# Stores of activations on SP, ten slots, shared wide buffers and early buffers beside the output projection

## The chip, the cores and the metric

The kernel runs on one core of a Trainium2 chip. The metric is device time in microseconds (us) of one execution, lower is better. The core has a matrix engine (TensorE, "PE" in the profile, with its weight loads as "PEld"), three engines for elementwise work (VectorE "DVE", ScalarE "ACT", GpSimd "POOL") and one that only issues transfers (SyncE "SP"). Every engine runs its own instructions strictly in order and waits on semaphores for the others. POOL, too, issues transfers, among them those that add to what lies at the destination ("accumulate").

## The reference

One decoder block on x of 512 tokens by 2048 channels, all in fp32. The part that matters here is the second half: the output projection of the mixers, and the gated MLP with its causal convolution of width 3.

```python
mix = concatenate([y_rwkv, y_pool]) @ w_out          # 2048 x 2048
x = x + gt1 * mix
h = rmsnorm(x, norm2_g) * (1 + sc2) + sh2

u = h @ w_up                                          # 2048 x 11264
y = conv_b + sum(conv_w[j] * shift(u, 2 - j) for j in range(3))
val, gate = split(y, 2)
x = x + gt2 * ((silu(gate) * val) @ w_down)           # 5632 x 2048
return rmsnorm(x, norm_f_g)
```

Ahead of it stand adaLN from c, the input projection, an RWKV-7 scan and a causal pooling mixer. None of that is touched.

## The kernel before

Channels lie on the 128 partitions and the 512 tokens in the free dimension; H0 and H1 are the two halves of 256 tokens. Each fp32 product is made of three matmuls (`mm3`, L118 to L122): operands are split into a rounded high part and the rest, and high×high (L120), high×low (L121) and low×high (L122) are summed in PSUM. So each weight tile needs a cast on ScalarE and a subtraction on VectorE before PE may use it: L113 and L115 for the earlier projections, L844 (`uhi`) and L846 (`ulo`) in `wsplit` for the up- and down-projection.

The stages, in the profile's time: the mixers up to some 785 us; the output projection (L769 to L818) up to some 985; the up-projection with convolution up to 2090; the down-projection to the end. The code is written as one stream, and a scheduler lays it out on the engines: it decides, per engine, in which order instructions stand, from which data and buffers they need. A pool's tag names a buffer; a new tile with a tag waits until the last user of the old one is done.

**Output projection.** `out_half(hf, f)` makes 128 output channels for one token half: four chunks of weights, each split by L113 and L115, then the residual and a store of x2 by POOL (L767). Loads of the mixers' outputs (`mxl`, L673) and their casts (`ah`, L141) feed it.

**Up-projection.** 88 blocks of 128 columns, in NF = 44 pairs j (a value block and its gate block). A pair's weights are two rows of 1 MB of `wup` (`row`, L855 to L860), row 0 = (w11, w12) and row 1 = (r1 base, w22), in four buffers x2_0 to x2_3 taken in turn, two per pair. So row 1 of one pair goes where row 1 of the pair two earlier lay, and may be loaded when its last reader, the subtraction of w22, is done. Each pair takes seven products in a scheme in the manner of Strassen, of 24 matmuls each: w11·Y11, w12·Y21, r1·T1, r2·T2, r4·Y22, r3·T3 and w22·T4. The activations T1 to T4, Y11, Y21, Y22 are sums and differences of h's quarters, split once (`combos`, L881 to L904). The weights' sums are made on the fly: r1 is row 1's right half plus an accumulate transfer by POOL (L967); r2 = r1 + w11 (VectorE, L991); r4 = r2 + w12 (L998); r3 is loaded by SP (L969) and accumulated by POOL (L970). w22·T4 of a pair is done in the next pair's iteration (`last_product`), since its row comes last; behind it `finish_pair` (L933 to L944) convolves u1 and u2 (L927 to L929), applies silu on ScalarE (L940), multiplies (L941), and POOL stores the result to `ad` in DRAM (L943). Partial sums leave PSUM by copies on ScalarE (L980, L989, L996; `cap`) and adds on VectorE (L985, L1000, L1009). These use `Slot`, a list of free buffers of 128×512 taken in the order in which they came free.

For the first NB = 10 pairs the first two products need only the first token half, so `first_two` (L866 to L877) makes them ahead, keeps them in DRAM (`early`), and the pair's iteration reads them back (L975) and takes five products instead of seven.

**Down-projection.** Two halves of 22 blocks; `act_pair` (L1027 to L1038) loads pairs of blocks of `ad`, casts (L1034) and subtracts (L1035) them into buffers freed by the up-projection (`ATAGS`); `down` loads weight rows (L1051) and splits them with `wsplit`.

Of the kernel before, what the change touches and what calls it, by code (L numbers as in the profile page):

```python
# [9 lines left out]
F32 = mybir.dt.float32  # L10
F32R = mybir.dt.float32r
# [5 lines left out]
P = 128  # L17
T = 512
D = 2048
KT = D // P  # L20
# [2 lines left out]
NC = 4  # L23
WC = 512
NWF = 8
NSLOT = 6
NB = 10
NJ = NF // 2
Q = float(np.exp(-0.5))
# [26 lines left out]
def block_kernel(ctx, tc, a, out, stop=None, dbg=None):  # L56
    nc = tc.nc
    V, S, G, PE = nc.vector, nc.scalar, nc.gpsimd, nc.tensor
# [65 lines left out]
    def project(ps, src, acts, start=True, stop=True, engs=(V,)):  # L124

        n = len(acts)
        for k0 in range(0, n, WC // P):
            wh, wl = split_weights(src[:, k0 * P : k0 * P + WC], engs[k0 // 4 % len(engs)])
            for kk in range(WC // P):
                k = k0 + kk  # L130
                sl = slice(kk * P, (kk + 1) * P)
                last = mm3(ps, wh[:, sl], wl[:, sl], *acts[k], start=start and k == 0, stop=stop and k == n - 1)
        return last
# [43 lines left out]
    if True:  # L177
# [28 lines left out]
        for k in range(KT):  # L206
            for part in (1, 0):
                j = part * 16 + k
# [9 lines left out]
            hi, lo = slots(k)  # L218
# [450 lines left out]
    M = []  # L669
# [35 lines left out]
    def half(acts, hf):  # L705
        sl = slice(hf * HT, (hf + 1) * HT)
        return [(h[:, sl], l[:, sl]) for h, l in acts]

    def wide(name):

        return rb.tile([P, 4, HT], F32, tag="wide", name=name, bufs=3)
# [57 lines left out]
    for f in range(8):  # L769
        out_done(f, pss[f], 0, T)  # L770

    def out_half(hf, f):
        ps = bank()[:, 0:HT]
        project(ps, a["wout"][f, :, :], half(M, hf))
        out_done(f, ps, hf * HT, (hf + 1) * HT)


# [7 lines left out]
    def split4(pool, tag, src):  # L785

        t = pool.tile([P, 2, 4, HT], F32R, tag=tag, name=tag)
        S.copy(t[:, 0, :, :], src)
        V.tensor_tensor(t[:, 1, :, :], src, t[:, 0, :, :].bitcast(F32), op=ALU.subtract)
        return t  # L790
# [13 lines left out]
    for f in range(8, KT):  # L804
        if f == 9:
            dg = norm_rows(acc[:, H0])
        if f == 10:
            rstd = norm_bcast(dg)
        if f >= 10:
            next(steps, None)  # L810
            if f % 2:
                next(steps, None)
        out_half(1, f)
    hctx.close()
    if stop == "B":
        return
# [11 lines left out]
    class Slot:  # L828
# [9 lines left out]
        def done(self):  # L838
            free.append(self.home)

    def wsplit(src):
        n = src.shape[-1]
        hi = ub.tile([P, 2 * QW], F32R, tag="whi", name="uhi", bufs=3)
        S.copy(hi[:, 0:n], src)  # L844
        lo = ub.tile([P, 2 * QW], F32R, tag="wlo", name="ulo", bufs=3)
        V.tensor_tensor(lo[:, 0:n], src, hi[:, 0:n].bitcast(F32), op=ALU.subtract)  # L846
        return hi, lo

# [8 lines left out]
    def row(n, pool, tag):  # L857
        t = pool.tile([P, 4 * QW], F32, tag=tag, name="wrow")
        nc.sync.dma_start(t, a["wup"][n, :, :])
        return t  # L860
# [4 lines left out]

    def first_two(n):  # L866

        w = row(2 * n, ub, f"t4{n % 2}")
        s_ = Slot("u1")
        ps = bank()[:, 0:HT]  # L870
        product(ps, w[:, W1], Y11)
        S.copy(s_[:, H1], ps)
        ps = bank()[:, 0:HT]
        product(ps, w[:, W2], Y21)
        V.tensor_add(s_[:, H0], s_[:, H1], ps)
        G.dma_start(early[n], s_.t)
        s_.done()  # L877
# [3 lines left out]
    def combos():  # L881
        for g in range(2):
            normed(g, H1, rstd)
            yield
            t = wide("t1")
            V.tensor_sub(t, x2q[g][:, :, H0], x2q[g][:, :, H1])
            T1[g] = split4(ub, f"t1{g}", t)
            yield
        for g in range(2):
            normed(g + 2, H1, rstd)  # L890
            yield
            t3 = wide("t3")
            V.tensor_sub(t3, x2q[g + 2][:, :, H1], x2q[g][:, :, H1])
            t2 = wide("t2")
            V.scalar_tensor_tensor(t2, t3, -1.0, x2q[g][:, :, H0], op0=ALU.mult, op1=ALU.subtract)
            yield
            T2[g] = split4(ub, f"t2{g}", t2)
            T3[g] = split4(ub, f"t3{g}", t3)
            yield
            Y22[g] = split4(ub, f"y22{g}", x2q[g + 2][:, :, H1])  # L900
            V.scalar_tensor_tensor(t2, t2, -1.0, x2q[g + 2][:, :, H0], op0=ALU.mult, op1=ALU.subtract)
            t4.append(t2)
            yield
# [12 lines left out]
    for _ in steps:  # L916
        pass
    for g in range(2):
        T4[g] = split4(ub, f"t4{g}", t4[g])
    free.append((rb, "acc"))  # L920

    ncw = rb.tile([P, 3, NF], F32, tag="ncw", name="ncw")
# [10 lines left out]
    def finish_pair(j, u1, u2):  # L933
        yv, yg = Slot("yv"), Slot("yg")
        conv(u1.t, yv.t, col("cw", j), col("cw", 88 + j), col("cw", 176 + j), col("cb", j))
        u1.done()

        conv(u2.t, yg.t, ncw[:, 0, j : j + 1], ncw[:, 1, j : j + 1], ncw[:, 2, j : j + 1], col("cb", 44 + j))
        u2.done()
        S.activation(yg.t, yg.t, AF.Silu)  # L940
        V.tensor_mul(yv.t, yv.t, yg.t)  # L941
        yg.done()
        G.dma_start(ad[j], yv.t)  # L943
        yv.done()  # L944

    pend = None
# [13 lines left out]
    for j in range(NF):  # L960
        w = []
        for i in range(2):
            w.append(row(2 * j + i, rb, f"x2_{(0, 2, 1, 3)[rows % 4]}"))
            rows += 1

        w11, w12, r1, w22 = w[0][:, W1], w[0][:, W2], w[1][:, W1], w[1][:, W2]
        G.dma_start(r1, a["wup"][2 * j + 1, :, W2], accum_op=ALU.add)  # L967
        r3 = ub.tile([P, 2 * QW], F32, tag="wr", name="r3", bufs=2)
        nc.sync.dma_start(r3, a["wup"][2 * j, :, W1])  # L969
        G.dma_start(r3, a["wup"][2 * j + 1, :, W1], accum_op=ALU.add)  # L970
        pa = bank()[:, 0:HT]
        cap = Slot("cap")
        if j < NB:
            u1 = Slot("u1")
            G.dma_start(u1.t, early[j])  # L975
            if pend:
                last_product(pend)
        else:
            product(pa, w11, Y11)
            S.copy(cap[:, H0], pa)  # L980
            last_product(pend)
            u1 = Slot("u1")
            pb = bank()[:, 0:HT]
            product(pb, w12, Y21)
            V.tensor_add(u1[:, H0], cap[:, H0], pb)  # L985
        u2 = Slot("u2")
        pc = bank()[:, 0:HT]
        product(pc, r1, T1)
        S.copy(cap[:, H1], pc)  # L989
        r2 = wide("r2").rearrange("p a b -> p (a b)")  # L990
        V.tensor_add(r2, r1, w11)  # L991
        product(pa, r2, T2, start=j < NB)
        if j < NB:
            V.tensor_add(cap[:, H0], u1[:, H1], pa)
        else:
            S.copy(cap[:, H0], pa)  # L996
        r4 = wide("r4").rearrange("p a b -> p (a b)")
        V.tensor_add(r4, r2, w12)  # L998
        product(pc, r4, Y22, start=False)
        V.tensor_add(u1[:, H1], cap[:, H0], pc)  # L1000
        if j < NB:
            pd = bank()[:, 0:HT]
            product(pd, r3, T3)
            V.tensor_add(u2[:, H1], cap[:, H0], cap[:, H1])
            V.tensor_add(u2[:, H1], u2[:, H1], pd)
            pend = (j, u1, u2, pd, w22, cap)
        else:
            product(pa, r3, T3, start=False)
            V.tensor_add(u2[:, H1], cap[:, H1], pa)  # L1009
            cap.done()  # L1010
            pend = (j, u1, u2, pa, w22, None)
# [10 lines left out]
        V.scalar_tensor_tensor(jk, wa, 1.0, cb, op0=ALU.mult, op1=ALU.mult, accum_out=mod[:, 80 + i : 81 + i])  # L1022

    ATAGS = [(rb, "y0"), (rb, "y1"), (rb, "y2"), (rb, "y3")]
    ATAGS += [(ub, f"{t}{g}") for t in ("t1", "t2", "y22", "t3", "t4") for g in range(2)]

    def act_pair(i):  # L1027

# [12 lines left out]
    def down_row():  # L1041
        nrow[0] += 1
        if nrow[0] % 5 < 2:
            return ub.tile([P, 2 * QW], F32, tag="wr", name="wd", bufs=2)
        return wide("wd").rearrange("p a b -> p (a b)")

    def down(ps, f, h, acts, blocks=(0, 8, 16)):
# [9 lines left out]
    def down_four(h, acts):  # L1057

        pss = [bank() for _ in range(4)]
        for k0 in (0, 8, 16):  # L1060
            for f in range(4):
                down(pss[f], f, h, acts, (k0,))
        return pss

    yd = [tc.dram_tile([P, T], F32, name=f"yd{f}") for f in range(KT)]
    A = []
    for i in range(NJ // 2):
        A += act_pair(i)
    for f in range(KT):
        if f == 0:  # L1070
            pss = down_four(0, A)
        ps = pss[f] if f < 4 else bank()
        if f >= 4:
            down(ps, f, 0, A)
        s_ = Slot("yd")
        S.copy(s_.t, ps)
        G.dma_start(yd[f], s_.t)
        s_.done()
        if f < 8:
            ada_gate2(2 * f)  # L1080
            ada_gate2(2 * f + 1)
# [2 lines left out]
    def gate(f):  # L1084
        return mod[:, 80 + f : 81 + f]

    A = []
    for i in range(NJ // 2, NJ):
        A += act_pair(i)
    x2q = [quad(i, "x2") for i in range(4)]  # L1090

    def load_x2(f):
# [140 lines left out]
```

## Time and profile before

| | us |
|---|---|
| median of the 3 runs shown (2594.88 to 2607.85) | 2604.18 |
| the profiled execution, its own time | 2610.18 |
| its span in the trace | 2608.1 |
| DVE waits for accumulated rows at L991 (42 times) | 195.9 |
| PE waits for the copy at L989 (33 times) | 95.3 |

In the profile, a row of an engine's timeline gives the start, the duration, the engine, the line, the operation, out<-in with the shape, and in brackets how long the engine idled before it and what released it. A row of the table of waits gives the waiting instruction, what ended its waits, the total, how many, and the longest.

Names of tiles in the profile lose their numbers, so all of r1's and w22's rows are `wrow`, r2, r3 and r4 are `r`, u1 and u2 are `u`, and a transfer `wrow<-wup` is SP's row load or POOL's accumulate.

### The profile page before, as it was taken

To read this page: it belongs to the slowest core of one execution; us is meant where nothing else is said; L and a number is where in the kernel's file an instruction comes from. 1 tells how busy PE (TensorE), PEld (TensorE's weight loads), DVE (VectorE), ACT (ScalarE), POOL (GpSimd) and SP (SyncE) were. 2 spreads that over 40 slices of the span, in tenths; PEclk is the share of its full clock that TensorE was granted. 3 is DMA by queue.
4 is the path that set the end of the run, shared out by engine and by line. 5 is a ranking of instruction groups with operands and counts; after the bars stand their busy time and mean duration, and the time that the engine had idled before them with its cause. 6 is when DMAs were issued, how large, how long until landed. Compare 5 with 4: busy or idle time off the path is not lost.

```text
span 2608.1 us, 42719 instructions
## 1 busy us (share of the span) xinstructions
PE 2357.0 (90%) x17122; PEld 2042.6 (78%) x17122; DVE 1641.9 (63%) x2648; ACT 1037.5 (40%) x1466; POOL 153.9 (6%) x237
## 2 busy tenths in 40 slices
PE   4789999999999999878889889889898999999997
PEld 3656666666668899777888889889888878877897
DVE  7987777777844567676656656656656674244355
ACT  3243444444333466333344444444444432232242
POOL 0000000000000101111000001001001001010000
PEclk9999999999999999989998999998999999999999
DMA  9965565566636568777555555565565687464365
GB/s 349 340 211 147 149 177 148 164 194 183 180 89 206 177 184 269 202 216 215 150 162 174 143 169 162 153 170 162 153 170 156 192 310 268 135 207 121 104 185 160
DMA packets 210873, 483.05 MB, mean 185 GB/s; under 512 B 73521, under 2 KB 79089, under 8 KB 191217
## 3 DMA queue, kind: packets, MB, share of 16 engines
q1 hardware_dynamic: 187634, 400.62, 48.4%
q0 software_dynamic: 23040, 79.71, 13.0%
q8 instruction: 134, 2.20, 0.3%
q14 instruction: 65, 0.53, 0.1%
HBM read 441.70 MB, written 38.54 MB: 184 GB/s over the span
## 4 chain that ended last, share of the span: by engine, by line
PE 27%; DMA 15%; issue 4%; DVE 4%; ACT 3%; SPq 0%; POOL 0%; ACTq 0%; POOLq 0%; DVEq 0%
DMA wrow<-wup 14%; PE b L120 9%; PE b L121 9%; PE b L122 9%; ACT uhi L844 2%; DVE ulo L846 2%; DVE yg L929 1%; DMA al<-ad 1%; ACT cap L989 0%; DMA yd<-yd 0%; DVE u L985 0%; DVE x L1108 0%; DMA ad<-yv 0%; SPq L1033 0%; DVE yv L941 0%
## 5 line engine op out<-in xcount | busy, mean ns | idle before, releaser
L122 PE MATMUL b<-t,ulo 128*128 128x256 f32 x1408 | 404.6, 288 | 32.1 <-DVE ulo L846 32.1
L120 PE MATMUL b<-t,uhi 128*128 128x256 f32 x1408 | 404.6, 287 | 10.8 <-ACT uhi L844 9.6
L120 PE MATMUL b<-y,uhi 128*128 128x256 f32 x1056 | 323.4, 306 | 97.7 <-ACT cap L989 95.3
L121 PE MATMUL b<-t,uhi 128*128 128x256 f32 x1408 | 403.4, 287 | 0.0
L122 PE MATMUL b<-y,ulo 128*128 128x256 f32 x1056 | 319.0, 303 | 2.2 <-DVE ulo L846 2.2
L121 PE MATMUL b<-y,uhi 128*128 128x256 f32 x1056 | 319.5, 303 | 0.0
L120 PE MATMUL b<-act,uhi 128*128 128x512 f32 (+1 forms) x880 | 307.4, 350 | 9.6 <-ACT act L1034 8.6
L121 PE MATMUL b<-act,uhi 128*128 128x512 f32 (+1 forms) x880 | 307.5, 350 | 0.5 <-DVE act L1035 0.5
L122 PE MATMUL b<-act,ulo 128*128 128x512 f32 (+1 forms) x880 | 307.4, 350 | 0.0
L120 PEld LDWEIGHTS b<-y,uhi 128*128 128x128 f32 x1056 | 222.9, 211 | 104.8 <-ACT cap L989 102.0
L122 PEld LDWEIGHTS b<-t,ulo 128*128 128x128 f32 x1408 | 275.3, 196 | 35.1 <-DVE ulo L846 35.0
L120 PEld LDWEIGHTS b<-t,uhi 128*128 128x128 f32 x1408 | 276.6, 197 | 12.2 <-ACT uhi L844 10.3
L844 ACT CAST uhi<-wrow 128x1024 fp32r<-128x1024 f32 x176 | 183.6, 1049 | 245.6 <-PE b L121 220.2
L121 PEld LDWEIGHTS b<-t,uhi 128*128 128x128 f32 x1408 | 275.5, 196 | 0.0
L846 DVE TENSOR_TENSOR ulo<-wd,uhi 128x1024 fp32r<-128x1024 f32 (+1 forms) x120 | 135.9, 1135 | 210.4 <-ACT uhi L844 201.5
L846 DVE TENSOR_TENSOR ulo<-wrow,uhi 128x1024 fp32r<-128x1024 f32 x176 | 214.8, 1224 | 79.9 <-ACT uhi L844 79.4
L113 ACT CAST whi<-wraw 128x512 fp32r<-128x512 f32 x236 | 145.7, 619 | 291.8 <-PE mm L121 120.4
L844 ACT CAST uhi<-wd 128x1024 fp32r<-128x1024 f32 (+1 forms) x120 | 117.3, 978 | 308.6 <-PE b L121 278.3
L115 DVE TENSOR_TENSOR wlo<-wraw,whi 128x512 fp32r<-128x512 f32 x236 | 161.6, 688 | 118.5 <-ACT whi L113 105.7
L122 PEld LDWEIGHTS b<-y,ulo 128*128 128x128 f32 x1056 | 221.6, 210 | 2.6 <-DVE ulo L846 2.6
L121 PEld LDWEIGHTS b<-y,uhi 128*128 128x128 f32 x1056 | 222.1, 210 | 0.0
L846 DVE TENSOR_TENSOR ulo<-r,uhi 128x1024 fp32r<-128x1024 f32 x132 | 161.2, 1222 | 59.7 <-ACT uhi L844 59.7
(309 smaller groups left out, 4661.3 us busy)
## 6 DMA issues: line engine op xcount, KB each, us to landing
wrow<-wup SPq DMA_DIRECT2D x98, 1024.0 KB, 7.2
wa<-ada SPq DMA_DIRECT2D x48, 1024.0 KB, 7.2
war<-ada SPq DMA_DIRECT2D x192, 256.0 KB, 3.5
wd<-wdn SPq DMA_DIRECT2D x80, 512.0 KB, 4.1
wraw<-win SPq DMA_DIRECT2D x140, 256.0 KB, 4.4
wraw<-wout SPq DMA_DIRECT2D x96, 256.0 KB, 3.4
r<-wup SPq DMA_DIRECT2D x44, 512.0 KB, 3.8
r<-wup POOLq DMA_DIRECT2D x44, 512.0 KB, 9.2
```

Of the source, the lines that this page charges most:

```text
L113: S.copy(hi, raw)
L115: eng.tensor_tensor(lo, raw, hi[:, :].bitcast(F32), op=ALU.subtract)
L120: PE.matmul(ps, wh, xh, start=start, stop=False, skip_group_check=more)
L121: PE.matmul(ps, wh, xl, start=False, stop=False, skip_group_check=more)
L122: return PE.matmul(ps, wl, xh, start=False, stop=stop, skip_group_check=more)
L844: S.copy(hi[:, 0:n], src)
L846: V.tensor_tensor(lo[:, 0:n], src, hi[:, 0:n].bitcast(F32), op=ALU.subtract)
L929: V.scalar_tensor_tensor(y[:, 2:T], u[:, 0 : T - 2], c0, y[:, 2:T], op0=ALU.mult, op1=ALU.add)
```

## The change

Six things are changed. Stores of `ad`, and the read of `early`, are issued by SP in place of POOL. The free list starts with ten slots in place of six (the accumulator's buffer makes eleven). A new pool `ea` is opened before the out-projection's pool closes, and holds two of the three sets of buffers of `wsplit`, and the rows of `first_two`, later T4 and two rows of down weights. r3 is taken from the `wide` buffers that r2 and r4 use, three in all, in place of a pair of its own. `combos` makes its four groups of operands in one loop. In the output projection's last six blocks, the subtraction L115 of every other chunk, twelve in all, stands on GpSimd. In the down-projection, activations are loaded inside `down_four`, eight blocks ahead of their use, and the first four blocks of the second half are loaded during the first.

```diff
-NSLOT = 6
+NSLOT = 10
-    def out_half(hf, f):
+    def out_half(hf, f, engs=(V,)):
-        project(ps, a["wout"][f, :, :], half(M, hf))
+        project(ps, a["wout"][f, :, :], half(M, hf), engs=engs)
-        out_half(1, f)
+        out_half(1, f, (V, G) if f >= 10 else (V,))
+
+    ea = ctx.enter_context(tc.tile_pool(name="ea", bufs=1, reuse_waits="tile"))
     hctx.close()
...
     def wsplit(src):
-        hi = ub.tile([P, 2 * QW], F32R, tag="whi", name="uhi", bufs=3)
+        pool, tag = ((ea, "0"), (ea, "1"), (ub, "2"))[nsplit[0] % 3]
+        nsplit[0] += 1
+        hi = pool.tile([P, 2 * QW], F32R, tag="whi" + tag, name="uhi")
         S.copy(hi[:, 0:n], src)
-        lo = ub.tile([P, 2 * QW], F32R, tag="wlo", name="ulo", bufs=3)
+        lo = pool.tile([P, 2 * QW], F32R, tag="wlo" + tag, name="ulo")
...
-        w = row(2 * n, ub, f"t4{n % 2}")
+        w = row(2 * n, ea, f"t4{n % 2}")
...
             T1[g] = split4(ub, f"t1{g}", t)
             yield
-        for g in range(2):
             normed(g + 2, H1, rstd)
...
-        T4[g] = split4(ub, f"t4{g}", t4[g])
+        T4[g] = split4(ea, f"t4{g}", t4[g])
...
-        G.dma_start(ad[j], yv.t)
+        nc.sync.dma_start(ad[j], yv.t)
...
-        r3 = ub.tile([P, 2 * QW], F32, tag="wr", name="r3", bufs=2)
+        r3 = wide("r3").rearrange("p a b -> p (a b)")
...
-            G.dma_start(u1.t, early[j])
+            nc.sync.dma_start(u1.t, early[j])
...
-    ATAGS += [(ub, f"{t}{g}") for t in ("t1", "t2", "y22", "t3", "t4") for g in range(2)]
+    ATAGS += [(ub, f"{t}{g}") for t in ("t1", "t2", "y22", "t3") for g in range(2)] + [(ea, "t40")]
+    wd2 = ea.tile([P, 2, 2 * QW], F32, tag="t41", name="wd2")
...
-            return ub.tile([P, 2 * QW], F32, tag="wr", name="wd", bufs=2)
+            return wd2[:, nrow[0] % 5, :]
...
         for k0 in (0, 8, 16):
+            while len(acts) < min(k0 + 8, NJ):
+                acts += act_pair((h * NJ + len(acts)) // 2)
             for f in range(4):
                 down(pss[f], f, h, acts, (k0,))
...
-    A = []
-    for i in range(NJ // 2):
-        A += act_pair(i)
+    A, A2 = [], []
...
+        if f == KT - 3:
+            A2 += act_pair(NJ // 2) + act_pair(NJ // 2 + 1)
...
-    A = []
-    for i in range(NJ // 2, NJ):
-        A += act_pair(i)
+    A = A2
```

The new lines shift the numbers by five or six in the up-projection: L846 becomes L852, L928 L933, L941 L946, L985 L990, L991 L996, L998 L1003.

The scheduler places some instructions elsewhere for it. On VectorE, in one iteration of the main up-projection loop, before the change (`yv` and `yg` are the convolved halves of the pair before, the numbers behind names tell tiles apart, r2_16497 belongs to the pair behind, and ulo_16329 is the rest of this pair's r3):

```order
L846 TENSOR_TENSOR ulo_16269<-r2_16265,uhi_16267 128x1024
L928 SCALAR_TENSOR_TENSOR yg_16193<-u2_16002,ncw_10646,yg_16193 128x511
L991 TENSOR_TENSOR r2_16497<-wrow_16358,wrow_16356 128x1024
L929 SCALAR_TENSOR_TENSOR yg_16193<-u2_16002,ncw_10646,yg_16193 128x510
L985 TENSOR_TENSOR u1_16203<-cap_16133,b_16204 128x256
L846 TENSOR_TENSOR ulo_16300<-r4_16296,uhi_16298 128x1024
L941 TENSOR_TENSOR yv_16192<-yv_16192,yg_16193 128x512
L998 TENSOR_TENSOR r4_16528<-r2_16497,wrow_16356 128x1024
L846 TENSOR_TENSOR ulo_16329<-r3_16129,uhi_16327 128x1024
L846 TENSOR_TENSOR ulo_16368<-wrow_16356,uhi_16366 128x1024
```

The same piece of VectorE's order with the change, up to the subtraction of w22 (ulo_16400):

```order
L852 TENSOR_TENSOR ulo_16272<-r2_16268,uhi_16270 128x1024
L933 SCALAR_TENSOR_TENSOR yg_16196<-u2_16005,ncw_10649,yg_16196 128x511
L934 SCALAR_TENSOR_TENSOR yg_16196<-u2_16005,ncw_10649,yg_16196 128x510
L990 TENSOR_TENSOR u1_16206<-cap_16136,b_16207 128x256
L852 TENSOR_TENSOR ulo_16303<-r4_16299,uhi_16301 128x1024
L946 TENSOR_TENSOR yv_16195<-yv_16195,yg_16196 128x512
L996 TENSOR_TENSOR r2_16500<-wrow_16361,wrow_16359 128x1024
L852 TENSOR_TENSOR ulo_16332<-r3_16132,uhi_16330 128x1024
L1003 TENSOR_TENSOR r4_16531<-r2_16500,wrow_16359 128x1024
L852 TENSOR_TENSOR ulo_16371<-wrow_16359,uhi_16369 128x1024
L1005 TENSOR_TENSOR u1_16206<-cap_16136,b_16238 128x256
L852 TENSOR_TENSOR ulo_16400<-wrow_16129,uhi_16398 128x1024
```

r2 of the pair behind, the first reader of the accumulated row, stood third in that piece and now stands seventh: behind both halves of the convolution, u1, the rest of r4 and the product yv. The rest of r3, which came after r4, now stands between r2 and r4.

On SP, with the change, at the loads of the output projection's operands (some 830 us in the profile before):

```order
L673 DMA mxl_8246<-mixd2_102 128x512
L673 DMA mxl_8252<-mixd3_103 128x512
L865 DMA wrow_9930<-wup 128x2048
L673 DMA mxl_8258<-mixd4_104 128x512
L673 DMA mxl_8264<-mixd5_105 128x512
```

The first row of the up-projection's weights (`wrow_9930`) stands between two loads of the mixers' outputs; before the change the loads stood one behind the other, and the row came only after that pool's end. On ScalarE its first cast now stands between those of ah9 and ah10:

```order
L141 CAST ah9_8254<-mxl_8252 128x512
L113 CAST whi_8230<-wraw_8228 128x512
L850 CAST uhi_9934<-wrow_9930 128x1024
L141 CAST ah10_8260<-mxl_8258 128x512
L850 CAST uhi_9964<-wrow_9930 128x1024
```

The casts of the weight row stand ahead of those of ah10 and ah11.

More of the change, by code (lines that the diff above doesn't have):

```diff
@@ L839, in done @@
             free.append(self.home)
+    nsplit = [0]
     def wsplit(src):
         n = src.shape[-1]
-        hi = ub.tile([P, 2 * QW], F32R, tag="whi", name="uhi", bufs=3)
+        pool, tag = ((ea, "0"), (ea, "1"), (ub, "2"))[nsplit[0] % 3]
+        nsplit[0] += 1
+        hi = pool.tile([P, 2 * QW], F32R, tag="whi" + tag, name="uhi")
         S.copy(hi[:, 0:n], src)
-        lo = ub.tile([P, 2 * QW], F32R, tag="wlo", name="ulo", bufs=3)
+        lo = pool.tile([P, 2 * QW], F32R, tag="wlo" + tag, name="ulo")
         V.tensor_tensor(lo[:, 0:n], src, hi[:, 0:n].bitcast(F32), op=ALU.subtract)
```

## The prediction

> **What bounds the kernel now.** I read the page first, then the table of waits, then the stretches, then single iterations.
>
> ```profile
> span 2608.1 us, 42719 instructions
> PE 2357.0 (90%) x17122; PEld 2042.6 (78%) x17122; DVE 1641.9 (63%) x2648; ACT 1037.5 (40%) x1466; POOL 153.9 (6%) x237
> PE 27%; DMA 15%; issue 4%; DVE 4%; ACT 3%; SPq 0%; POOL 0%; ACTq 0%; POOLq 0%; DVEq 0%
> DVE r L991 <- DMA wrow<-wup: 195.9, 42, 7.8
> PE b L120 <- ACT cap L989: 95.3, 33, 5.0
> POOL ad L943 <- DVE yv L941: 416.2, 43, 19.7
> 1269.05:2055.32 786.27, 696.05 (x5377) 689.56 (x5377) 481.05 (x546) 332.48 (x449) 73.04 (x96) 0.93 0.57 161
> ```
>
> PE counts as 90% busy, but a transfer of wup rows is 14 points of the chain, and two waits repeat once per pair: VectorE's add r2 (L991) waits for the accumulated row, and PE's first matmul of the product with r4 waits for the copy L989. The longest wait, POOL's for the store, is no bound: nothing behind it is ready earlier (below). The last row is the main up-projection loop, from the first such PE wait to the last of them: us, busy time of PE, PEld, DVE, ACT, POOL, granted clock, DMA share, GB/s.
>
> ```profile
> 1269.05 0.58 PE L120 MATMUL b<-y,uhi 128*128 128x256 f32 x1 [5.05 <-ACT cap L989]
> 2055.32 0.58 PE L120 MATMUL b<-y,uhi 128*128 128x256 f32 x1 [2.59 <-ACT cap L989]
> 1722.97 0.28 PE L121 MATMUL b<-y,uhi 128*128 128x256 f32 x1
> 1723.09 0.28 PE L122 MATMUL b<-y,ulo 128*128 128x256 f32 x1
> ```
>
> Both ends are the same matmul of pairs 32 iterations apart, so one pair takes 786.27/32 = **24.57 us**. Matmuls start every 0.12 us when nothing stops them; a pair has 7 products of 24, so 168 × 0.12 = **20.16 us** is the least PE can do. The difference, 4.4 us a pair or 141 us in all, is what can be won here. Of it 95.3 us is the wait itself; the rest is the slower clock (0.93 in that row) after each wait.
>
> One iteration, in order of time, shows what closes the circle:
>
> ```profile
> 1694.39 1.23 DVE L846 TENSOR_TENSOR ulo<-wrow,uhi 128x1024 fp32r<-128x1024 f32 x1
> 1695.64 3.32 SPq L859 DMA_DIRECT2D wrow<-wup  x2
> 1701.72 0.85 POOL L967 DMA_DIRECT2D wrow<-wup  x1 [5.42 <-DVE ulo L846]
> 1710.42 1.23 DVE L991 TENSOR_TENSOR r<-wrow 128x1024 f32<-128x1024 f32 x1 [5.45 <-DMA wrow<-wup]
> 1711.57 0.74 DVE L929 SCALAR_TENSOR_TENSOR yg<-u,ncw,yg 128x510 f32<-128x510 f32 x1
> 1712.40 0.63 ACT L940 ACTIVATE yg<-yg 128x512 f32<-128x512 f32 x1 [6.48 <-DVE yg L929]
> 1712.94 1.03 ACT L844 CAST uhi<-r 128x1024 fp32r<-128x1024 f32 x1
> 1713.88 0.36 ACT L989 COPY cap<-b 128x256 f32<-128x256 f32 x1
> 1714.29 0.58 PE L120 MATMUL b<-y,uhi 128*128 128x256 f32 x1 [3.58 <-ACT cap L989]
> 1718.61 1.05 ACT L844 CAST uhi<-wrow 128x1024 fp32r<-128x1024 f32 x1 [3.15 <-PE b L121]
> 1719.69 1.23 DVE L846 TENSOR_TENSOR ulo<-wrow,uhi 128x1024 fp32r<-128x1024 f32 x1 [0.47 <-ACT uhi L844]
> ```
>
> The subtraction for w22 frees a row buffer; SP loads the next odd row into it; POOL accumulates the other row onto its half; r2 may be added: 1710.42 − 1695.62 = 14.8 us. Only then the conv's L929 behind r2 on VectorE, the silu and the cast of r3 behind L929 on ScalarE, the copy L989 behind these, and PE: 3.9 us from r2 to PE. Then 4.3 us of slowed matmuls before a buffer lets the cast of w22 begin, 2.3 us for cast and subtraction, and the ring is closed: 14.8 + 3.9 + 4.3 + 2.3 = 25.3 us (1695.62 to 1720.92). **PE waits for a copy that only stands behind work that waits for a DMA.**
>
> **The change: order of the main loop.** In the changed order r2 stands behind both L929s, the add u1, ulo(r4) and the product yv. So L929, silu, cast and copy no longer wait for the accumulate, and PE's wait at r4 goes. What is late next is the row ring itself, now wholly on VectorE. The rows that price it are the next iteration's r2, VectorE's add u1, and the stretch of the first ten pairs:
>
> ```profile
> 1734.63 1.23 DVE L991 TENSOR_TENSOR r<-wrow 128x1024 f32<-128x1024 f32 x1 [4.41 <-DMA wrow<-wup]
> 1718.80 0.42 DVE L1000 TENSOR_TENSOR u<-cap,b 128x256 f32<-128x256 f32 x1 [1.02 <-PE b L122]
> 1172.00:1251.00 79.00, 65.46 (x496) 63.95 (x497) 51.95 (x68) 29.56 (x36) 11.28 (x16) 0.94 0.72 203
> 1188.65 2.13 SPq L859 DMA_DIRECT2D wrow<-wup  x2
> 1203.36 1.23 DVE L991 TENSOR_TENSOR r<-wrow 128x1024 f32<-128x1024 f32 x1 [4.53 <-DMA wrow<-wup]
> 1208.48 2.13 SPq L859 DMA_DIRECT2D wrow<-wup  x2
> ```
>
> From r2 to the end of ulo(w22) VectorE does r2, ulo(r3), r4, ulo(w11) and ulo(w22), each 1.14 us from start to start (r2 above: 1710.42 to 1711.57), and u1, 0.42 with its overlap taken off 0.35: 6.05 us. The transfer part was 14.8 us above and 13.7 in the next iteration (1720.92 to 1734.63), at 161 GB/s. At a shorter period the same bytes give 161 × 24.57/20.6 = 192 GB/s; the stretch of the first ten pairs has 203 GB/s and took 14.7 us (1188.65 to 1203.36). I take 14.5. Ring: 14.5 + 6.05 = **20.6 us**, just over PE's 20.16. That a ring of this kind sets a pace of its own, that stretch shows: 19.83 us a pair (1188.65 to 1208.48), where five products would let PE do with 120 × 0.12 = 14.4. The gain is 32 × (24.57 − 20.6) = **−127 us**; at PE's own limit −140, and at 22 us (a transfer part of 15.9, over these three) −82.
>
> **Stores of ad on SP.** The 43 waits of 416 us in all leave POOL. They held nothing: at 1701.72 the accumulate starts on its landed row, POOL having idled 5.42 us. On SP the store stands behind the base load of r3 and ahead of the next odd row; it waits for L941, which VectorE now does before r2, while the odd row needs ulo(w22), 6 us after. Nothing; if L941 came late, every us would go into the ring.
>
> **r3 from the wide buffers.** Its base load now waits until ulo of the r3 before is done, where it had a second buffer.
>
> ```profile
> 1716.68 0.33 SPq L969 DMA_DIRECT2D r<-wup  x1
> 1720.86 0.86 POOL L970 DMA_DIRECT2D r<-wup  x1 [5.61 <-DMA r<-wup]
> r<-wup POOLq DMA_DIRECT2D x44, 512.0 KB, 9.2
> ```
>
> That ring: 4.2 (base), 9.2 (accumulate), 1.05 + 1.14 (cast, subtraction), some 15.6 us, 5 below the period. Nothing.
>
> **First pairs, and the out-projection.** Split operands in a pool of their own beside the earlier stage, twelve subtractions L115 on POOL, and the copy loop in one pass bear on these waits of PE:
>
> ```profile
> 951.18 0.39 PE L122 MATMUL b<-ah,wlo 128*128 128x256 f32 x1 [2.10 <-DVE wlo L115]
> 986.09 0.39 PE L120 MATMUL b<-y,uhi 128*128 128x256 f32 x1 [1.96 <-ACT uhi L844]
> 1049.16 0.58 PE L120 MATMUL b<-t,uhi 128*128 128x256 f32 x1 [4.83 <-ACT uhi L844]
> ```
>
> These three come to 8.9 us; as in the main loop, where 95.3 us of waits cost 141, that makes 13. The odd row of an early pair also goes out earlier in the changed order. I take −15, between 0 and −30, twice that. The subtractions on POOL have no row in this trace: its nearest are the memset of 128x1024 at 0.96 us and VectorE's own L115 at 0.69, so about 1 us each, twelve in all, among stores that leave POOL waiting:
>
> ```profile
> L331 POOL MEMSET xy<- 128x1024 f32 x1 | 1.0, 959 | 0.0
> L115 DVE TENSOR_TENSOR wlo<-wraw,whi 128x512 fp32r<-128x512 f32 x236 | 161.6, 688 | 118.5 <-ACT whi L113 105.7
> 935.85 0.54 POOL L767 DMA_DIRECT2D x2d<-x  x1 [5.22 <-DVE x L740]
> ```
>
> A library load stands ahead of the first; 5.2 us of idle time cover it, and I take nothing, up to +5. By the Trainium skill, GPSIMD Engine Reference, Instruction dispatch, the first call of a freshly loaded kernel pays about 6 us; no run here shows it, and by it the sum would be 1 to 3 us longer. The first wup row (1 MB) now loads amid the out-projection, and its cast stands before that of ah10:
>
> ```profile
> wrow<-wup SPq DMA_DIRECT2D x98, 1024.0 KB, 7.2
> ```
>
> That can cost from nothing to a row's whole landing, 7.2 us, if ScalarE stands there for it; of that a third, +2.5, since the queue ahead of it holds only small loads.
>
> **Down projection.** Blocks of eight activations need not all be cast before the first matmul, and the second half's first four are loaded ahead:
>
> ```profile
> L120 PE MATMUL b<-act,uhi 128*128 128x512 f32 (+1 forms) x880 | 307.4, 350 | 9.6 <-ACT act L1034 8.6
> 2349.26 0.79 PE L120 MATMUL b<-act,uhi 128*128 128x512 f32 x1 [6.53 <-ACT act L1034]
> ```
>
> PE waits 8.6 us for casts of activations, 6.53 of them at the second half's start; with the slowed matmuls behind, by the loop's ratio, 12.7. I take −9 (0 to −13).
>
> Sum: −127 − 15 + 2.5 − 9 = **−148.5 us**. The profiled execution took 2610.18 (2.1 outside its span), 6.0 above the median of the runs shown, 2604.18: 2461.7 for one like it, **2456** for the median.
>
> **Rivals.**
> 1. Denser traffic makes the ring 22 us: −82 in place of −127, **2501**. For it: the transfer part is two transfers in a row on DMA engines already 57% busy. Against it: the 203 GB/s stretch. Between this and the forecast nothing is sharp.
> 2. The stall only moves: a transfer part of 18 us gives a period of 24, 18 saved in place of 127, **2565**. Against it: the highest of the three transfer parts read is 14.8. The same time would come if the new order did not act as I read it, with another wait holding the copy.
> 3. Slower: r3's single buffer. Its ring is 6.4 + the accumulate's time. Over 42 pairs of both kinds it decides from a period of 23.6 on (there 32 × (24.57 − 23.6) = 31 and the 6.5 of the other terms meet 10 × (23.6 − 19.8) = 38), so from an accumulate of 17 us, 1.9 times the median 9.2. At 18.4 us, twice the median: period 24.8, +7 in the loop, +50 in the first ten pairs, −6.5 else, **2655**. For it: it becomes dearer just when queues fill. Against: it needs doubling in every pair.
>
> **How the numbers follow.** Forecast 0.58 (2425 to 2485), rival 1 0.22, rival 2 0.13, rival 3 0.07. Low end: PE's limit −140, −30, 0 and −13 give −183, so 2421, and some us for the spread of runs (the lowest shown is 9 under the median): 2415. High end: −82 + 0 + 7 + 5 + 0 gives −70, so 2534, with a part of rival 2: 2545. A change under 0.5% (13 us) can't be told from none: the lower end of rival 2 and the edge of rival 3, 0.02 each, so 0.04. Slower by more: the rest of rival 3, 0.05. Faster: 0.58 + 0.22 + 0.11 = 0.91.
>
> **What would show it.** Right: PE's wait on the copy (L994 there) falls from 95 us to under 15; the spacing of pairs is 20 to 21 us; the clock of the loop nears 1.00; VectorE waits at r2 (L996) still, with PE seldom behind it. Rival 1 shows r2's wait longer and PE waiting for uhi or ulo of r2; rival 3 shows the cast of r3 waiting for its accumulate. Wrong would be a loop above 22 us a pair, or PE waits in the out-projection on wlo from POOL over 5 us.

## The result and the profile after

| | us |
|---|---|
| before, median of 4 runs (2594.88 to 2610.99) | 2606.01 |
| changed, median of 4 runs (2434.23 to 2441.24) | 2438.97 |
| ratio, 95% interval | 0.9362 [0.9328, 0.9397] |
| predicted | 2456 (2415 to 2545) |

The changed kernel is 167 us faster, 19 us more than the 148.5 that the sum gave. Its page, in the lines that answer to those of before, and the main loop, from the same two matmuls (the first of r4 in the first pair with seven products, and that of 32 pairs later):

```profile
span 2439.2 us, 42721 instructions
PE 2295.3 (94%) x17122; PEld 1986.5 (81%) x17122; DVE 1643.0 (67%) x2636; ACT 1039.9 (43%) x1466; POOL 139.7 (6%) x195
PE 77%; DVE 9%; DMA 7%; issue 4%; ACT 3%; SPq 0%; POOL 0%; DVEq 0%; POOLq 0%; ACTq 0%
1248.87:1888.56 639.69, 639.69 (x5378) 639.69 (x5377) 487.04 (x545) 337.44 (x448) 55.48 (x65) 1.00 0.71 198
```

PE is busy for all of the 639.69 us, at a granted clock of 1.00 (0.93 before): 639.69/32 = **19.99 us a pair**, where it took 24.57. In the chain that ended last, the transfers of wup rows fell from 14% to 3%, and PE rose from 27% to 77%. PE's waits for the copy (L989, now L994), 95.3 us before, are gone from the table of waits, and of VectorE's 195.9 us of waits for accumulated rows 8.6 are left, ahead of the loop (nine more waits of the same add there, 26.9 us, have no releaser that the profile shows).

To see where else time went, each trace is cut at four marks: M, the matmul of the output projection behind PE's wait of 0.94 us for a residual (882.96 before, 881.69 after; what lies ahead is the same code and drifts by up to 11 us between profiles), the two matmuls of r4 above, and the end of the span. The tables take the stretches between them from each trace.

| us | M to first r4 | 32 pairs | rest | M to end |
|---|---|---|---|---|
| before | 386.1 | 786.3 | 552.7 | 1725.1 |
| changed | 367.2 | 639.7 | 550.6 | 1557.5 |
| difference | −18.9 | −146.6 | −2.1 | −167.6 |

One iteration of the changed kernel, in order of time, on SP, POOL and VectorE:

```profile
1701.24 1.23 DVE L852 TENSOR_TENSOR ulo<-r,uhi 128x1024 fp32r<-128x1024 f32 x1 [1.59 <-ACT uhi L850]
1702.49 0.33 SPq L974 DMA_DIRECT2D r<-wup  x1
1705.90 1.22 DVE L996 TENSOR_TENSOR r<-wrow 128x1024 f32<-128x1024 f32 x1
1706.74 0.86 POOL L975 DMA_DIRECT2D r<-wup  x1 [6.76 <-DMA r<-wup]
1707.04 1.22 DVE L852 TENSOR_TENSOR ulo<-r,uhi 128x1024 fp32r<-128x1024 f32 x1
1712.65 1.22 DVE L852 TENSOR_TENSOR ulo<-wrow,uhi 128x1024 fp32r<-128x1024 f32 x1 [0.47 <-ACT uhi L850]
1713.90 3.26 SPq L865 DMA_DIRECT2D wrow<-wup  x2
1719.13 0.86 POOL L972 DMA_DIRECT2D wrow<-wup  x1 [11.52 <-DMA wrow<-wup]
```

r2 (L996) starts without a wait. The odd row is issued at 1713.90, behind the subtraction of w22, and its accumulate 5.2 us later. r3's base load goes out at 1702.49, 0.02 us after the subtraction of r2 ends (1701.24 + 1.23), and its accumulate at 1706.74, 7 us ahead of the odd row. Before, r3's accumulate (1720.86) and the odd row's load (1720.95) started together. The summary of transfers in the middle of the loop (1300 to 1850 us; issues, KB, median us to landing), first of before, then of the change:

```profile
wrow<-wup SPq DMA_DIRECT2D x46, 1024.0 KB, 7.5
r<-wup POOLq DMA_DIRECT2D x23, 512.0 KB, 9.1
wrow<-wup POOLq DMA_DIRECT2D x23, 512.0 KB, 7.6
```

```profile
wrow<-wup SPq DMA_DIRECT2D x54, 1024.0 KB, 4.9
wrow<-wup POOLq DMA_DIRECT2D x28, 512.0 KB, 5.7
r<-wup POOLq DMA_DIRECT2D x28, 512.0 KB, 5.5
```

All three land sooner, though the traffic rose from 161 to 198 GB/s. The first row of each summary mixes odd rows with even ones, which are issued 2.9 us behind them, so it is not what the ring pays. Taken issue by issue from the traces over the same stretch (medians of the time from issue to landing), the odd row takes 5.6 us before and 4.8 with the change, the even one 8.2 and 5.0; from the odd row's issue to the landing of its accumulate it is 14.1 us before and 11.1 with the change. In the iteration above, the odd row (1713.90) and its accumulate (1719.13) have these landings:

```profile
DMA to landing us min/median/max: 4.7/4.7/4.7
DMA to landing us min/median/max: 5.6/5.6/5.6
```

The accumulate thus lands at 1724.7, and the next r2 starts at 1725.90. So two things differ in the loop, VectorE's order and the times of r3's transfers, and the change has six parts that could have made them. The experiments take these apart.

### The profile page after: what moved, and what is told of

It reads as the page before. It is cut to its first block, busy times and chain, and to the rows that moved or that the text cites. A ratio compares the mean times of both kernels' runs of the same rounds, so it can differ in the third digit from the quotient of the medians.

```text
span 2439.2 us, 42721 instructions
## 1 busy us (share of the span) xinstructions
PE 2295.3 (94%) x17122; PEld 1986.5 (81%) x17122; DVE 1643.0 (67%) x2636; ACT 1039.9 (43%) x1466; POOL 139.7 (6%) x195
## 4 chain that ended last, share of the span: by engine, by line
PE 77%; DVE 9%; DMA 7%; issue 4%; ACT 3%; SPq 0%; POOL 0%; DVEq 0%; POOLq 0%; ACTq 0%
PE b L122 18%; PE b L120 18%; PE b L121 18%; PE mm L121 3%; PE mm L120 3%; PE mm L122 3%; DMA wrow<-wup 3%; DVE jk L212 2%; DVE ulo L852 1%; PE pb L537 1%; DMA war<-ada 1%; PE pb L535 1%; DMA wraw<-win 1%; PE pb L528 1%; PE pa L298 1%
## 5 line engine op out<-in xcount | busy, mean ns | idle before, releaser
L120 PE MATMUL b<-y,uhi 128*128 128x256 f32 x1056 | 298.0, 282 | 1.3 <-ACT uhi L850 1.3
L122 PE MATMUL b<-y,ulo 128*128 128x256 f32 x1056 | 298.0, 282 | 0.4 <-DVE ulo L852 0.3
L121 PE MATMUL b<-y,uhi 128*128 128x256 f32 x1056 | 297.9, 282 | 0.0
L120 PEld LDWEIGHTS b<-t,uhi 128*128 128x128 f32 x1408 | 272.8, 194 | 4.1 <-ACT act L1040 2.8
L852 DVE TENSOR_TENSOR ulo<-wd,uhi 128x1024 fp32r<-128x1024 f32 (+1 forms) x120 | 136.1, 1135 | 205.3 <-ACT uhi L850 202.0
L121 PEld LDWEIGHTS b<-t,uhi 128*128 128x128 f32 x1408 | 272.5, 194 | 0.0
L852 DVE TENSOR_TENSOR ulo<-wrow,uhi 128x1024 fp32r<-128x1024 f32 x176 | 214.7, 1222 | 81.8 <-ACT uhi L850 81.8
L115 DVE TENSOR_TENSOR wlo<-wraw,whi 128x512 fp32r<-128x512 f32 x224 | 156.2, 700 | 108.0 <-ACT whi L113 92.3
L850 ACT CAST uhi<-r 128x1024 fp32r<-128x1024 f32 x132 | 138.5, 1049 | 171.0 <-PE b L121 165.5
L120 PEld LDWEIGHTS b<-y,uhi 128*128 128x128 f32 x1056 | 200.4, 190 | 1.7 <-ACT uhi L850 1.7
L122 PEld LDWEIGHTS b<-y,ulo 128*128 128x128 f32 x1056 | 199.9, 189 | 0.8 <-DVE ulo L852 0.8
L852 DVE TENSOR_TENSOR ulo<-r,uhi 128x1024 fp32r<-128x1024 f32 x132 | 160.9, 1220 | 57.9 <-ACT uhi L850 57.9
```

Of the source, the lines that this page charges most:

```text
L115: eng.tensor_tensor(lo, raw, hi[:, :].bitcast(F32), op=ALU.subtract)
L120: PE.matmul(ps, wh, xh, start=start, stop=False, skip_group_check=more)
L121: PE.matmul(ps, wh, xl, start=False, stop=False, skip_group_check=more)
L122: return PE.matmul(ps, wl, xh, start=False, stop=stop, skip_group_check=more)
```

## The experiments

**One part alone: the order, r3's buffers, the stores.** Three kernels start from the kernel before. In the first, only VectorE's order is changed, by holding r2 behind a product that was traced a pair earlier; the orders of the other engines and all buffers stay:

```diff
-        V.tensor_mul(yv.t, yv.t, yg.t)
+        muls.append(V.tensor_mul(yv.t, yv.t, yg.t))
...
-        V.tensor_add(r2, r1, w11)
+        with tc.issue_after(muls[-2].ins) if j > NB else ExitStack():
+            V.tensor_add(r2, r1, w11)
```

> The kernel before, with one thing changed: the add r2 of the next pair is held behind the product yv of the pair before, so VectorE's order in the main loop is that of the changed kernel, while SP's, POOL's and ScalarE's orders and all buffers stay as before. Theory A (the order alone lifts the stall): the main loop goes from 24.57 to between 20.0 and 20.6 us a pair, PE's wait for the copy L989 from 95 us to under 15, the time to 2460 to 2485. Theory B (the transfers became shorter because r3 is loaded at another time, and the order is secondary): with r3 loaded as before, the ring keeps its transfer part of over 14.5 us and the loop stays above 22 us, the time above 2520. Theory C (the stall only moves to another wait): 24 us, about 2590.

The second takes r3 from the wide buffers and nothing else. VectorE's order in the loop then comes out as in the changed kernel, by the scheduler:

```diff
-        r3 = ub.tile([P, 2 * QW], F32, tag="wr", name="r3", bufs=2)
+        r3 = wide("r3").rearrange("p a b -> p (a b)")
```

> The kernel before, with r3 taken from the three wide buffers and nothing else: VectorE's order becomes the new one and r3 is loaded in its own pair's iteration, half a period after its row instead of beside the next. Theory A: a loop of 20.0 to 20.6 us a pair, 2455 to 2480, within 10 us of the run with the order alone. Theory B: a loop of 20.0 where the order alone has over 22, so at least 60 us faster than that run. If the other parts (store on SP, ten slots) carry the loop, it stays above 22 here too.

The third has only the stores of ad on SP (`G.dma_start(ad[j], yv.t)` becomes `nc.sync.dma_start(ad[j], yv.t)`):

> The kernel before with only the stores of ad issued by SP. Its orders on VectorE are those of before. Expected by the prediction's step: no difference, 2595 to 2615; POOL's 416 us of waits for yv go. If POOL's wait held the accumulate back, the transfer part falls by up to 1 us a pair and the time by 30 us; if the store holds the odd row back on SP, the time rises by as much.

And one starts from the changed kernel and undoes r3's buffers, and with them the ten slots (six again, to make room):

> The changed kernel with r3 back in two buffers of its own (and six slots, which makes room for them): VectorE's order goes back to that of before. Theories A and B alike: the loop back at 23.5 to 24.6 us a pair and about 2575 to 2590, PE waiting for the copy some 90 us; if stores on SP or slots carry the loop, under 22 and below 2500.

| | time, us | ratio to before [95%] | M to first r4 | a pair | rest |
|---|---|---|---|---|---|
| before | 2607.29 | | 386.1 | 24.57 | 552.7 |
| order alone | 2463.66 | 0.9453 [0.9429, 0.9477] | 376.9 | 20.42 | 550.6 |
| r3's buffers alone | 2442.44 | 0.9373 [0.9345, 0.9401] | 366.4 | 20.15 | 550.1 |
| stores alone | 2608.69 | 1.0004 [0.9992, 1.0017] | 384.9 | 24.55 | 553.4 |
| changed, r3 as before (one run) | 2602.43 | | 375.3 | 24.84 | 550.5 |
| changed | 2438.97 | 0.9362 [0.9328, 0.9397] | 367.2 | 19.99 | 550.6 |

Theory A holds: the order alone gives 20.42 us a pair. Theory C falls, and so does B as it stood, which wanted over 22 us there; what is left for it is the remainder below. **One line, r3's buffers, makes nearly the whole gain**: alone it gives 0.9373, and the other parts without it (the ten slots are undone there too) leave the kernel at 2602. Two expectations were missed here. That last run was to take 2575 to 2590 us: its other stretches are 10.8 and 2.2 us shorter than before, but its loop is 8.6 us longer, and why was not looked into. And r3's buffers alone were to stay within 10 us of the order alone, but are 21 us below it. The line acts through the order that the scheduler then makes on VectorE, and a second time by something that the order alone lacks: 20.42 against 20.15 in the loop, and 10 us ahead of it. The store on SP moves nothing, as predicted. In the run with the order alone the iteration reads as the prediction had it:

```profile
1687.64 1.23 DVE L993 TENSOR_TENSOR r<-wrow 128x1024 f32<-128x1024 f32 x1 [3.98 <-DMA wrow<-wup]
1693.77 3.24 SPq L859 DMA_DIRECT2D wrow<-wup  x2
1694.37 0.86 POOL L971 DMA_DIRECT2D r<-wup  x1 [9.83 <-DMA r<-wup]
1708.60 1.23 DVE L993 TENSOR_TENSOR r<-wrow 128x1024 f32<-128x1024 f32 x1 [4.09 <-DMA wrow<-wup]
1259.39:1912.78 653.39, 649.59 (x5378) 646.46 (x5377) 477.17 (x544) 337.33 (x448) 73.21 (x96) 1.00 0.69 195
```

r2 to the odd row's issue is 6.1 us (6.05 in the sum), from there to the next r2 14.8 us (14.5 in the sum), r2 still waits for the transfer, and PE is short of work for 653.39 − 649.59 = 3.8 us in the whole loop. The accumulate of r3 (1694.37) still runs beside the odd row (1693.77).

**The time of r3's transfers.** The order alone, with a single buffer of r3's own:

```diff
-        r3 = ub.tile([P, 2 * QW], F32, tag="wr", name="r3", bufs=2)
+        r3 = ub.tile([P, 2 * QW], F32, tag="wr", name="r3", bufs=1)
```

> The kernel with the order alone (r2 held behind yv), and r3 in a single buffer of its own in place of two; the two buffers' places still serve the down-projection's weight rows. r3 is now loaded in its own pair's iteration, as in the run with r3 from the wide buffers, but still after the subtraction of the r3 before, so its accumulate still falls beside the next odd row's load. If the time at which r3's transfers run is what separates the order alone (20.42 us a pair) from the shared buffers (20.15), the loop stays at 20.3 to 20.6 here, and the row's landing at about 7 us; if it is the lead of a pair, or one buffer fewer, it becomes 20.1, with a landing of about 5. If a single buffer binds (the prediction's rival of the slower side) it rises above 22.

It took 20.24 us a pair, one run, 2458.03 us: between the two values that were to be told apart, and nearer to the 20.15 of the shared buffers. The time of this one run therefore does not decide. The transfers do more; their summary over the same stretch:

```profile
wrow<-wup SPq DMA_DIRECT2D x55, 1024.0 KB, 7.1
r<-wup POOLq DMA_DIRECT2D x27, 512.0 KB, 8.7
```

From the odd row's issue to the landing of its accumulate it is 14.1 us, as with the order alone (14.2) and before (14.1), against 11.1 in both kernels that have r3 in the wide buffers. The landings stay long while r3 is issued behind its own subtraction, so one buffer fewer, or a load in its own pair, is not what shortened them; a single buffer does not bind either. In the kernels with 14 us r3's accumulate lands some 3 us after the row's accumulate is issued, in the other two 6 us ahead of it; whether the row's accumulate is held up by that one, or both by the row loads, was not taken apart. Then the changed kernel, with 512 KB more to load per pair, at two places (and eight slots for ten):

```diff
+        r3d = nc.sync.dma_start(r3, a["wup"][2 * j, :, W1])
+        if j > NB:
+            with tc.issue_after(r3d.ins):
+                nc.sync.dma_start(scr, a["wup"][2 * j, :, W1])
```

> The changed kernel with an extra load of 512 KB of wup per pair in the main loop, read by nobody, issued right behind r3's base load (eight slots in place of ten make room for it). If it matters when transfers run, not how many bytes: no odd row is under way then, the row's landing stays near 5 us, the loop stays at 20.0 to 20.2 and the time within 8 us of 2439. If the amount of traffic sets the pace, the loop goes to 21 to 22 us, the time to 2470 to 2505.

For the other place the same load hangs on the odd row's:

> The same extra 512 KB per pair, but issued right behind the odd row's load, so that it runs beside the one transfer of the ring. If it matters when transfers run: the row's landing goes from 4.9 us to 6.5 to 8, r2 waits again, the loop goes to 20.6 to 22 us and the time to 2455 to 2500, at the same bytes as the run with the load behind r3. If the amount alone counts, both runs have the same loop. If the ring has more slack than I think, both stay at 20.0.

Behind r3's base load (medians of landing: odd and even rows, accumulate onto the row), then beside the odd row:

```profile
wrow<-wup SPq DMA_DIRECT2D x54, 1024.0 KB, 4.8
...
wrow<-wup POOLq DMA_DIRECT2D x27, 512.0 KB, 5.5
```

```profile
wrow<-wup SPq DMA_DIRECT2D x54, 1024.0 KB, 5.9
...
wrow<-wup POOLq DMA_DIRECT2D x27, 512.0 KB, 6.8
```

Loops: 19.99 and 20.02 us a pair, times 2436.39 and 2438.14 (two runs each), both within the spread of the changed kernel. The loops thus do not tell the two apart: the expected 20.6 to 22 us for the second place was wrong. The landings do. From the odd row's issue to the landing of its accumulate it is 11.1 us with the load at the first place, as in the changed kernel without it, and 12.5 at the second, at the same bytes (225 and 224 GB/s in the loops). The difference of 1.4 us is nearly all the accumulate's (5.5 and 6.8); the higher median of the row loads, 5.9, comes from the even rows. So the place of a transfer in time decides what it costs the ring, and not the bytes alone. The loop does not show it because in the changed kernel r2 starts a median of 0.9 us after its accumulate has landed; with the load at the second place 0.1 us of that is left.

**What is left: the down-projection's start.** The rest of the kernel, expected 9 us shorter, was 2.1 shorter. PE waits there for one cast:

```profile
1927.57 0.79 PE L120 MATMUL b<-act,uhi 128*128 128x512 f32 x1 [5.90 <-ACT uhi L850]
1921.70 0.81 SPq L1057 DMA_DIRECT2D wd<-wdn  x2
```

The first weight row needed lies where T4 was (`wd2`), and its load goes out at 1921.70, when the last product with T4 is over. With `nrow = [1]` for `nrow = [0]` the rotation starts one row later, and the first rows go to the wide buffers:

> The changed kernel with the rotation of down weight rows started one later, so that the first rows needed go to the wide buffers and not to the one that lies where T4 was, which is free only after the last product of the up-projection. In the changed kernel PE waits 5.90 us at 1927.57 for the cast of that row. If that wait is due to the buffer: it goes, with the slowed matmuls behind it, 4 to 8 us, a time of 2431 to 2435. If another load is as late, no difference, 2439.

2432.19 us (2428.29 to 2435.57, 5 runs) against 2438.97, and the rest of the kernel goes from 550.6 to 542.1 us: the wait of 5.90 us is gone. The intervals of the two ratios (0.932 [0.9299, 0.9341] and 0.9362 [0.9328, 0.9397]) overlap a little, so the gain rests on the trace more than on the times. The next runs all start from this kernel.

**The pool ea, GpSimd, and the pairs ahead.** In the first, ea is opened behind `hctx.close()`, on that pool's side; in the second, `out_half(1, f)` uses VectorE alone; the third and fourth have NB = 8 and NB = 6.

> The changed kernel with the later rotation of down weight rows, and the pool ea opened after the out-projection's pool is closed, on its side: the same buffers at other addresses, and the first rows of wup loaded only behind the last rows of wout, as before the change. Two questions. The early loads: if the first product waits again at the seam, the start of the first products comes 2 to 6 us later than 984, if not it is hidden. The pitch: in the runs with ea beside the out-projection one matmul of 128x256 follows the other after 118.99 ns in the main loop and one of 128x512 after 232.5 ns in the down-projection, in the others after 119.9 and 229.6. If the addresses of the split buffers set it, both go to the others' values (loop 20.14 us a pair, +5 us; down-projection some 5 us shorter); if the code around them does, they stay.

> The changed kernel with the later rotation of down weight rows and all subtractions of the output projection back on VectorE. The trace of the changed kernel has five gaps of PE of 1.1 to 1.7 us on low parts of weights in that stretch (before: two, 2.4 and 2.2). If GpSimd's 1.28 us for each is what PE waits for, the gaps return to two and the stage ends 0 to 4 us earlier; if VectorE is the tighter engine there, it ends 2 to 6 us later. Time within 6 us of 2432.

> The changed kernel with the later rotation of down weight rows and eight in place of ten pairs whose first two products are made ahead. Now that a pair of the main loop takes 20.0 us, one of the first ten costs 19.6 in its iteration and 5.76 for its two products ahead, 25.4. If that holds, two fewer save 2 x 5.4 = 10.7 us: 2420 to 2424. If the second token half's operands are not ready two pairs earlier (VectorE is busy there), PE waits for them and the gain is 0 to 5 us.

> The same with six pairs ahead. If each pair less saves 5.4 us: 2410 to 2415. If PE waits for the second half's operands (their work on VectorE and ScalarE is the same, in 23 us less of PE's time): no faster than eight pairs, 2420 to 2435.

| | time, us | M to first r4 | a pair | rest |
|---|---|---|---|---|
| later rotation | 2432.19 | 366.6 | 19.99 | 542.1 |
| + ea after the pool ahead | 2444.09 | 375.0 | 20.15 | 540.2 |
| + no GpSimd subtractions | 2432.04 | 365.6 | 19.99 | 542.3 |
| + eight pairs ahead | 2422.20 | 357.3 | 19.99 | 543.4 |
| + six pairs ahead | 2427.29 | 362.4 | 19.99 | 543.8 |

Without the early place PE waits 6.07 us at the seam for the first cast of wup, and the stretch up to the loop is 8.4 us longer, more than the 2 to 6 expected; the kernel before, whose first row is as late, waits 1.96 us there, and the difference was not traced. GpSimd's twelve subtractions are worth nothing that shows: PE's waits for low parts of w_out are 4.2 us in the kernel before (all for VectorE) and 5.2 in the changed one:

```profile
L122 PE MATMUL b<-ah,wlo 128*128 128x256 f32 x256 | 72.9, 285 | 5.2 <-POOL wlo L115 2.7 <-DVE wlo L115 2.5
```

Eight pairs ahead are faster than both kernels: **2422.20 us (2420.21 to 2428.26), 0.9306 [0.928, 0.9332]**, 10 us below the same kernel with ten, close to the 10.7 worked out. The traces, from M to the end, give 8.1 us (1548.4 and 1540.3), and the intervals of these two ratios overlap, so the size is known to some us only. With six, PE waits 8.44 us at the first product with T1, for the cast of an accumulated row that waits for its landing (and not, as was expected, for the second half's operands), and by the medians half of the gain is gone.

## Why the prediction was right

**The bound, and the order of the loop.** Right, and shown: holding r2 behind yv, with nothing else, took the loop from 24.57 to 20.42 us where the ring was worked out at 20.6, with 6.1 and 14.8 us for its two parts. PE's wait at the copy went, as said; VectorE's wait at r2 stayed in that run. In the changed kernel it did not stay, against what the prediction named as a sign of being right: the loop there is bound by PE and no longer by the ring.

**The term that was too small: −127, measured −146.6.** The step that failed is the one on r3's buffers. It said that r3's base load waits for the subtraction of the r3 before, costs nothing, and changes nothing. The load waits for the subtraction of r2, by the times above, which is done 4.6 us before r3's even begins (1702.47 against 1707.04), so that r3's accumulate no longer runs beside the odd row. The transfer part of the ring, from the odd row's issue to the landing of its accumulate, is then 11.1 us, where the sum had 14.5 and the kernel with the order alone has 14.2; the ring falls below PE's time, and PE's own 20 us set the pace. I had carried the transfer part over from before, though the change moves the transfers; the rows of both accumulates' issue were there to be laid beside each other. Of the 19.6 us, about 6 are the ring with the order alone (20.42 for 20.6), 9 lie between that and r3's buffers alone (20.15), and 5 between those and the changed kernel (19.99), which are PE's pitch (last section): the least of 20.16 us that the prediction gave PE was not the least. That r3's time shortens the landings is borne out by the kernel with the same order and r3 at its old time (14.1 us) and by the load added at two places. How much of the 9 us it makes is less sure, since the single buffer took two thirds of them in its one run; a run in which r3 alone was moved back within the changed kernel was not made.

**First pairs and out-projection: −15 + 2.5, measured −18.9.** The reason was another than the one given. r3's buffers alone give −19.7; the other parts without them −10.8, and they do not add. GpSimd gives none, and the first weight row among the loads ahead costs nothing that shows. The library load, taken as nothing, is hidden: GpSimd's first subtraction starts 4.1 us after the store ahead of it ends, and its idle time there is ended by ScalarE's cast of its weights:

```profile
934.58 0.54 POOL L767 DMA_DIRECT2D x2d<-x  x1 [5.22 <-DVE x L740]
939.19 1.28 POOL L115 TENSOR_TENSOR wlo<-wraw,whi 128x512 fp32r<-128x512 f32 x1 [4.08 <-ACT whi L113]
```

The figure of about 6 us (the Trainium skill, GPSIMD Engine Reference, Instruction dispatch) would have put it at 941 us or later; here it took less, or was paid elsewhere.

**Down-projection: −9, measured −2.1.** The 6.53 us at the second half did go, but the weight row in T4's buffer cost 5.90 at the start, which the prediction did not see. With the later rotation the rest is 10.6 us shorter than before, so the term was sound for what it looked at. It is luck that this error (+6.9) and that of the first pairs (−6.4) cancel in the sum; what is left is the loop's.

**Stores and rivals.** The store on SP is worth 1.0004 [0.9992, 1.0017], so nothing. Rival 1 (denser traffic) did not come: with the order alone, at 195 GB/s, the transfer part is 14.2 us where it was 14.1 at 161, and in the changed kernel, at 198, it is shorter. Rival 2 (the stall only moves) wanted 24 us a pair. Rival 3 (r3's buffer binds) is far off even with a single buffer, 20.24 us a pair.

## What to carry to other kernels

A buffer decides more than memory: through the time at which it comes free, one line on r3's buffers moved the scheduler's order on another engine and took two transfers apart, and was worth nearly all of a change with six parts. When a change moves a transfer, price the ring's transfers anew, from what will then run beside them, and not from the old landings. And once the main loop is PE-bound, look again at what was made ahead to shorten it: two pairs fewer ahead gave 8 to 10 us.

## What was not expected of the hardware

PE's pitch, the time from one matmul's start to the next, changed between kernels that differ in the place of the buffers. In the stretches below PE is busy throughout at a clock of 1.00, with the same instructions: r3's buffers alone, the later rotation, and the same with ea at other addresses:

```profile
1246.77:1891.46 644.69, 644.69 (x5378) 644.69 (x5377) 487.91 (x547) 337.25 (x448) 74.57 (x98) 1.00 0.70 197
```

```profile
1249.28:1888.97 639.69, 639.69 (x5379) 639.69 (x5377) 487.03 (x546) 337.55 (x448) 55.17 (x64) 1.00 0.71 198
```

```profile
1258.19:1902.88 644.69, 644.69 (x5378) 644.69 (x5377) 487.84 (x546) 337.22 (x448) 55.50 (x65) 1.00 0.70 196
```

A pair takes 19.99 us with the split weights in ea beside the pool ahead and 20.15 us elsewhere; the first comes back to the hundredth in six kernels, the second in two, and both were seen on the same chip. So the last 5 us of the loop's gain go, as far as these runs tell, with addresses: the run that moved ea, and with it what lies behind on that side and the time of the first loads, lost them. In the down-projection it is the other way: from start to start of matmuls of 128x512, 232.5 ns on average between 2100 and 2300 us with ea beside the pool ahead, and 230.1 with it moved; the rest of that kernel is 1.9 us shorter for it, where 5 were expected. Which operand's address does it, weights or activations, was not tried.
